# Feed-forward input in pairs of column blocks by seven block products, in a sequence written by hand

## The chip, the core and the metric

The kernel runs on one core of a Trainium2 chip. The metric is the device time of one execution in microseconds (us). The core's engines each work through a queue of their own, in order: TensorE (PE, with its weight loads as PEld), VectorE (DVE), ScalarE (ACT), GpSimd (POOL) and SyncE (SP, which only issues transfers here). They wait for each other by semaphores.

## What is computed

A layer of a decoder trunk, for one batch of 256 tokens:

```python
# S = 256 tokens, D = 1024, FFN_HIDDEN = 2816; one layer
xn = rmsnorm(h, norm_mix_g)
q_a, k_a, v_a, q_b, f_b, i_b, og_b, g_a, g_b = split_cols(xn @ w_in)     # nine blocks of 1024 columns
y_a = moba_attention(q_a, k_a, v_a, positions) @ w_br_attn               # 16 heads of 64, rotary, causal
y_b = hgrn2(q_b, f_b, i_b, og_b, lb, hgrn_norm_g) @ w_br_hgrn            # 8 heads of 128, gated recurrence
h = h + (sigmoid(g_a) * y_a + sigmoid(g_b) * y_b) @ w_out
h = h + memory_cross_attention(rmsnorm(h, norm_x_g), rmsnorm(mem, norm_mem_g), wq_x, wkv_x, wo_x)
hn = rmsnorm(h, norm_ffn_g)
gu = hn @ w_ffn_in                                                       # 1024 x 5632
h = h + (silu(gu[..., :2816]) * gu[..., 2816:]) @ w_ffn_out              # 2816 x 1024
return rmsnorm(h, final_norm_g)
```

## The kernel before

All weights are float32. For accuracy each matrix product is made of three: a weight chunk `raw` is split into a rounded part `hi` (ScalarE copies it to float32r) and a remainder `lo = raw - hi`, the activations likewise, and TensorE adds x_hi*w_hi, x_hi*w_lo and x_lo*w_hi in PSUM (`mm3t`, lines 236 to 239).

The weights are cut into 97 chunks of 1 MB (128 x 2048), laid out in DRAM in the order of their use (`plan`). `prep` loads a chunk on SP's queue into one of two `raw` buffers and splits it in two halves of 1024 columns: ScalarE makes `hi` (line 193); of `lo` (line 197) VectorE takes 576 columns of a half and GpSimd 448, but for the first nine chunks, where VectorE takes all. `nxt` hands out the next chunk and prepares two further ones; `hi` and `lo` have three buffers each. A chunk costs TensorE 24 matmuls of 512 columns.

Stages in order: the nine blocks of `w_in`, with recurrence and attention between them; the two branch outputs and `w_out`; cross-attention with `wkv_x`, `wq_x` and `wo_x`; the feed-forward, chunks 64 to 96. The last one's 2816 hidden columns are eleven blocks `o` of 256. Block `o` has two input chunks ("I", o, kh), one for each half kh of the 1024 features, each with 256 gate columns beside 256 value columns, and one output chunk ("O", o). For each token half t (128 tokens) the input chunks add into one PSUM bank `psi`; `gate` makes silu(r * gate) on ScalarE and the product with r * value on VectorE (`fu`), where r is the row scale of the norm. `turn_hid` turns the 256 x 256 block by four transposes into a bank `hidT` and splits it into `hid`, one of six buffers. `out_part` adds `hid` times the output chunk to four accumulators `acc`, which stay in PSUM to the end. Banks come from two pools of four: `mm` for psi, hidT and the like, `sm` for acc and smaller things. In the feed-forward the order on TensorE is I(o,0), turn(o-1), I(o,1), O(o-1):

```python
for u in ORDER[at[0]:-2]:
    if u[0] == "O":
        ffn_out(u[1])
        continue
    _, o, kh = u
    w = by_k(nxt(), 4)
    for t in range(2):
        ffn_in(o, kh, t, w)
        ...
        if kh == 1:
            gate(o, t)
    if kh == 0 and o:
        turn_hid(o - 1)
```

TensorE's queue stands as the code is written (a manual schedule). The other engines' queues are ordered by the scheduler from the code, except at the opening on GpSimd and in the closing sequence (final norm and output), which are written out by hand.

Of the kernel before, what the change touches and what calls it, by code (L numbers as in the profile page):

```python
# [10 lines left out]
F32 = mybir.dt.float32  # L11
F32R = mybir.dt.float32r
# [54 lines left out]


ORDER = plan()


def lay(ws):
# [45 lines left out]
def build(tc, A, out):  # L118
    nc = tc.nc
    V, SC, G, PE, SY = nc.vector, nc.scalar, nc.gpsimd, nc.tensor, nc.sync  # L120
    with ExitStack() as ctx:
# [14 lines left out]
        def t2(name, shape=(128, 512)):  # L136
            return ta.tile(list(shape), F32, name=name, tag="ta")
# [30 lines left out]
        def prep(tags=None, raw=None):  # L168
            i = made[0]
            made[0] += 1  # L170
            first = i < 2
            if raw is None:
                raw = wr.tile([128, 2048], F32, name="raw", tag="raw")
            if tags is None:
                hi = wh.tile([128, 2048], F32R, name="hi", tag="hi")
                lo = wl.tile([128, 2048], F32R, name="lo", tag="lo")
            else:
                hi = big(tags[0], "hix", (128, 2048), F32R)
                lo = big(tags[1], "lox", (128, 2048), F32R)
            pieces = 4 if first else 2  # L180
            n = 2048 // pieces
            sent = PIECES[i] if i < len(PIECES) else 1
            for c in range(sent if 0 < i < len(PIECES) else 0):
                a = slice(c * 2048 // sent, (c + 1) * 2048 // sent)
                SY.dma_start(raw[:, a], piece(A["w"][i], a))
            if sent == 1:
                SY.dma_start(raw, A["w"][i])
            for c in range(pieces):
                a = slice(c * n, (c + 1) * n)
                if i == 0:  # L190
                    SY.dma_start(raw[:, a], piece(A["w"][i], a))
                    yield
                SC.activation(hi[:, a], raw[:, a], AF.Copy)  # L193
                cut = (c + 1) * n - (0 if i in ALONE else POOL_COLS // pieces)
                for eng, b in ((V, slice(c * n, cut)), (G, slice(cut, (c + 1) * n))):
                    if b.start < b.stop:
                        eng.tensor_tensor(lo[:, b], raw[:, b], hi[:, b].bitcast(F32), op=ALU.subtract)  # L197
            ready[i] = (hi, lo)

        def run(g):  # L200
            for _ in g:
                pass

        def nxt(lead=LEAD):
            i = at[0]
            at[0] += 1
            while made[0] <= min(i + lead, len(ORDER) - 1):
                run(prep())
            return ready.pop(i)


# [24 lines left out]
        def mm3t(ps, xh, xl, h, l, first, last):  # L236
            PE.matmul(ps, xh, h, start=first, stop=False)  # L237
            PE.matmul(ps, xh, l, start=False, stop=False)  # L238
            PE.matmul(ps, xl, h, start=False, stop=last)  # L239

        def by_k(w, k):
            return tuple(t.rearrange("p (k c) -> p k c", k=k) for t in w)
# [819 lines left out]
        def wo_part(ps, t, c, kh):  # L1062
            t_part(ps, wo[2 * c + kh], (oxh, oxl), t, kh)

        def turn_h2(t, c):
# [7 lines left out]
            SC.activation(h2h[:, ks, ts], g, AF.Copy)  # L1073
            G.tensor_tensor(h2l[:, ks, ts], g, h2h[:, ks, ts].bitcast(F32), op=ALU.subtract)
# [12 lines left out]

        ring = ("B7", "B14", "B10", "B11", "B12", "B6")
        X2 = (h2h, h2l)
        hid, acc, two, psi, hm = {}, {}, {}, {}, {}  # L1090

        def gate(o, t):
            r, ps = two["r"][:, t:t + 1], psi.pop((o, t))
            g = t2("fg", (128, 256))
            SC.activation(g, ps[:, 0:256], AF.Silu, scale=r)  # L1095
            u = t2b("fu", (128, 256))
            V.scalar_tensor_tensor(u, ps[:, 256:512], r, g, op0=ALU.mult, op1=ALU.mult)  # L1097
            hm[o, t] = u

        def turn_hid(o):  # L1100
            bk = mm.tile([128, 2, 256], F32, name="hidT", tag="mm")
            for t in range(2):
                u = hm.pop((o, t))
                for j in range(2):
                    PE.transpose(bk[:, j, t * 128:(t + 1) * 128], u[:, j * 128:(j + 1) * 128], ident)
            hd = big(ring[o % 6], "hid", (128, 2, 2, 256), F32R)
            split(bk, hd[:, 0], hd[:, 1])
            hid[o] = hd

        def ffn_in(o, kh, t, w):  # L1110
            if kh == 0:
                psi[o, t] = mm.tile([128, 512], F32, name="psi", tag="mm")
            t_part(psi[o, t], w, X2, t, kh)

        def out_part(o, w, t, c, home=None, u=0, v=512):
            if home is None and (t, c) not in acc:
# [8 lines left out]
        def ffn_out(o):  # L1125
            w = by_k(nxt(), 2)
            for t in range(2):
                for c in range(2):
                    out_part(o, w, t, c)

        for u in ORDER[at[0]:-2]:
            if u[0] == "O":
                ffn_out(u[1])
                continue
            _, o, kh = u
            w = by_k(nxt(), 4)
            for t in range(2):
                ffn_in(o, kh, t, w)
                if (o, kh, t) == (0, 0, 0):
                    turn_h2(1, 1)  # L1140
                    two["r"] = rstd2(ssq2, "h2")
                if kh == 1:
                    gate(o, t)
            if kh == 0 and o:
                turn_hid(o - 1)

        n = NF // 2 - 1
        wa = by_k(nxt(), 2)  # L1150
        wb = by_k(nxt(), 2)
        out_part(n - 1, wa, 0, 0)
        turn_hid(n)
# [12 lines left out]
        hg3 = {i: big(ring[j], "hg3", (128, 512)) for j, i in enumerate(((0, 0), (0, 1), (1, 0)))}  # L1166
# [18 lines left out]
        def send(eng, t, u, w):  # L1185
            eng.dma_start(out[t * 128:(t + 1) * 128, u:w], H[:, t, u:w])

        E = mybir.EngineType
        with tc.manual_schedule(engines={E.Activation, E.DVE, E.Pool, E.SP}):
            add_out(acc[0, 0], 0, 0, 512)  # L1190
            mean_part(0, 0, 0, 512)
            gain(0, 0)
            add_out(acc[0, 1], 0, 512, 1024)
            mean_part(1, 0, 512, 1024)
            gain(0, 1)
            add_out(acc[1, 1], 1, 512, 1024)
            V.tensor_scalar(v3[:, 0:1], ssq3[:, 0:1], ssq3[:, 1:2], EPS, op0=ALU.add, op1=ALU.add)
            power(0, 0)
            SC.activation(H[:, 0, 0:512], hg3[0, 0], AF.Copy, scale=rs[0])
            send(SY, 0, 0, 512)  # L1200
            add_out(acc[1, 0], 1, 0, 512)
            mean_part(2, 1, 0, 512)
            gain(1, 0)
            for i in range(2):
                add_out(ends[i], 1, 512 + 256 * i, 768 + 256 * i)
                mean_part(3 + i, 1, 512 + 256 * i, 768 + 256 * i)
            V.tensor_scalar(H[:, 0, 512:1024], hg3[0, 1], rs[0], None, op0=ALU.mult)
            send(SY, 0, 512, 1024)
            V.tensor_scalar(v3[:, 1:2], ssq3[:, 2:3], ssq3[:, 3:4], EPS, op0=ALU.add, op1=ALU.add)
            V.tensor_scalar(v3[:, 2:3], ssq3[:, 4:5], v3[:, 1:2], None, op0=ALU.add)  # L1210
            power(1, 2)
            SC.activation(H[:, 1, 0:512], hg3[1, 0], AF.Copy, scale=rs[1])
            send(SC, 1, 0, 512)
            for i in range(2):
                a = slice(512 + 256 * i, 768 + 256 * i)
                V.scalar_tensor_tensor(H[:, 1, a], H[:, 1, a], rs[1], gfin[:, a], op0=ALU.mult, op1=ALU.mult)
                send(SY, 1, a.start, a.stop)


# [42 lines left out]
```

## Time and profile before

| | |
|---|---|
| device time, median of 3 runs | 626.13 us (625.99 to 626.78) |
| the profiled execution: span from first to last instruction | 624.0 us; the page gives no time of it beside the span |
| instructions in the span | 8466 |
| TensorE, weight loads | 615.9 us busy (99%), 512.5 us (82%) |
| VectorE, ScalarE, GpSimd | 384.2 us (62%), 331.4 us (53%), 372.4 us (60%) |
| moved by DMA | 107.50 MB, mean 172 GB/s |
| feed-forward on TensorE | from 432 us on |

A row of a group reads: line, engine, operation, output <- inputs, shapes, count, then busy us and mean ns of one, then the idle time of the engine just before them and what ended it. A row of a timeline or of the chain in order of time begins with its start and its length in us. A row of a table by stage has the stretch, the busy us (and instructions) of each engine, the granted clock, the DMA queues' share and GB/s. A matmul's record is its whole passage; the next one starts before it has ended.

### The profile page before, as it was taken

The page shows a single profiled execution, that of the slowest core. Times are in us where ns is not written, and L with a number is a line of the kernel's source. Part 1 is how long each engine was busy: PE and PEld are TensorE (multiplying, and loading weights), DVE is VectorE, ACT ScalarE, POOL GpSimd, SP SyncE. Part 2 cuts the span into 40 slices and gives each one's busy share as a digit, 9 for nine tenths or more (in the row PEclk, how much of TensorE's full clock was granted, in tenths as well). Part 3 has the DMA queues.
Part 4 walks back from the last instruction along what each step waited for, and adds up shares of the span by engine and source line. Part 5 has one row for each costly group of instructions (what it writes and reads, how often), then busy time and mean ns, then how long its engine had stood idle before and what let it go on. Part 6 is the DMA issues. An engine that isn't in the chain of part 4 may idle for free.

```text
span 624.0 us, 8466 instructions
## 1 busy us (share of the span) xinstructions
PE 615.9 (99%) x3135; PEld 512.5 (82%) x3135; DVE 384.2 (62%) x672; ACT 331.4 (53%) x533; POOL 372.4 (60%) x296
## 2 busy tenths in 40 slices
PE   9999999999999999999999999999999999999995
PEld 7888888888877877778888889888888888888884
DVE  7566678979766875748856456754444444444433
ACT  7775554234376756727457556644543444434432
POOL 3887844556544464355867876656655665566553
PEclk9999999999999999999999999999999999999998
DMA  9755443334443333545455544453344555454511
GB/s 345 296 204 202 155 182 135 135 135 140 185 149 135 136 135 134 204 169 183 156 207 189 183 175 189 140 199 134 132 178 171 195 203 187 166 190 198 203 68 67
DMA packets 16888, 107.50 MB, mean 172 GB/s; under 512 B 2000, under 2 KB 2640, under 8 KB 4560
## 3 DMA queue, kind: packets, MB, share of 16 engines
q1 hardware_dynamic: 16128, 106.14, 46.5%
q10 hardware_dynamic: 720, 0.84, 0.4%
q8 instruction: 24, 0.39, 0.3%
q14 instruction: 16, 0.13, 0.1%
HBM read 105.92 MB, written 1.05 MB: 171 GB/s over the span
## 4 chain that ended last, share of the span: by engine, by line
PE 98%; DVE 0%; POOL 0%; issue 0%; POOLq 0%; DVEq 0%
PE pst L237 14%; PE pst L239 14%; PE pst L238 14%; PE psi L237 6%; PE psi L239 6%; PE psi L238 6%; PE psf L252 5%; PE acc L237 3%; PE acc L239 3%; PE acc L238 3%; PE psf L253 2%; PE lp L616 2%; PE psg L510 1%; PE pso L237 1%; PE pso L239 1%; PE pso L238 1%
## 5 line engine op out<-in xcount | busy, mean ns | idle before, releaser
L197 POOL TENSOR_TENSOR lo<-raw,hi 128x448 fp32r<-128x448 f32 x172 | 272.6, 1602 | 182.1 <-ACT hi L193 169.6
L193 ACT ACTIVATE hi<-raw 128x1024 fp32r<-128x1024 f32 (+1 forms) x194 | 195.7, 1036 | 165.9 <-PE pst L239 58.9
L197 DVE TENSOR_TENSOR lo<-raw,hi 128x576 fp32r<-128x576 f32 (+2 forms) x194 | 198.1, 1027 | 133.6 <-ACT hi L193 131.6
L237 PE MATMUL pst<-hi,Xh 128*128 128x512 f32 x256 | 103.2, 403 | 0.0
L239 PE MATMUL pst<-hi,Xl 128*128 128x512 f32 x256 | 99.9, 390 | 0.0
L238 PE MATMUL pst<-lo,Xh 128*128 128x512 f32 x256 | 99.8, 390 | 0.0
L237 PE MATMUL psi<-hi,h2h 128*128 128x512 f32 x176 | 69.6, 395 | 0.0
L239 PE MATMUL psi<-hi,h2l 128*128 128x512 f32 x176 | 68.7, 390 | 0.0
L238 PE MATMUL psi<-lo,h2h 128*128 128x512 f32 x176 | 68.5, 389 | 0.0
L239 PEld LDWEIGHTS pst<-hi,Xl 128*128 128x128 f32 x256 | 48.0, 188 | 10.4
L237 PEld LDWEIGHTS pst<-hi,Xh 128*128 128x128 f32 x256 | 48.1, 188 | 9.9 <-issue 0.7
L238 PEld LDWEIGHTS pst<-lo,Xh 128*128 128x128 f32 x256 | 48.1, 188 | 9.3
L239 PEld LDWEIGHTS psi<-hi,h2l 128*128 128x128 f32 x176 | 33.0, 188 | 7.1
L238 PEld LDWEIGHTS psi<-lo,h2h 128*128 128x128 f32 x176 | 33.1, 188 | 6.6
L237 PEld LDWEIGHTS psi<-hi,h2h 128*128 128x128 f32 x176 | 33.1, 188 | 6.5
L237 PE MATMUL acc<-hi,hid 128*128 128x512 f32 x86 | 33.6, 390 | 0.0
L239 PE MATMUL acc<-hi,hid 128*128 128x512 f32 x86 | 33.5, 389 | 0.0
L238 PE MATMUL acc<-lo,hid 128*128 128x512 f32 x86 | 33.5, 389 | 0.0
L1097 DVE SCALAR_TENSOR_TENSOR fu<-psi,r_h,fg 128x256 f32<-128x256 f32 x22 | 10.6, 484 | 26.0 <-ACT fg L1095 26.0
L1095 ACT ACTIVATE fg<-psi,r_h 128x256 f32<-128x256 f32 x22 | 10.4, 475 | 29.9 <-PE psi L239 29.9
L252 PE MATMUL psf<-H,hi 128*128 128x512 f32 x64 | 22.8, 400 | 0.0
L252 PE MATMUL psf<-M,hi 128*128 128x512 f32 x64 | 22.5, 396 | 0.0
(344 smaller groups left out, 1120.9 us busy)
## 6 DMA issues: line engine op xcount, KB each, us to landing
raw<-w SPq DMA_DIRECT2D x94, 1024.0 KB, 4.8
raw<-w SPq DMA_DIRECT2D x4, 512.0 KB, 6.1
raw<-w SPq DMA_DIRECT2D x4, 256.0 KB, 4.1
H<-xtok SPq DMA_DIRECT2D x1, 1024.0 KB, 9.2
mraw<-mT SPq DMA_DIRECT2D x1, 1024.0 KB, 5.0
xraw<-xT SPq DMA_DIRECT2D x1, 512.0 KB, 6.1
gfin<-gfin SPq DMA_DIRECT2D x1, 512.0 KB, 3.7
out<-H SPq DMA_DIRECT2D x2, 256.0 KB, 2.0
```

The lines of the kernel that those rows point to most:

```text
L193: SC.activation(hi[:, a], raw[:, a], AF.Copy)
L197: eng.tensor_tensor(lo[:, b], raw[:, b], hi[:, b].bitcast(F32), op=ALU.subtract)
L237: PE.matmul(ps, xh, h, start=first, stop=False)
L238: PE.matmul(ps, xh, l, start=False, stop=False)
L239: PE.matmul(ps, xl, h, start=False, stop=last)
L252: PE.matmul(ps, w[0][:, k, a], X2[:, :, k], start=k == 0, stop=False)
L253: PE.matmul(ps[:, 0], w[1][:, k, a], X2[:, 0, k], start=False, stop=k == 7)
L510: PE.matmul(pss[c][t], z[:, k, t * 128:(t + 1) * 128], ws[c][0][:, k], start=z is Xh and k == 0, stop=False)
L616: PE.matmul(ps[:, j], KS[:, a0 + j], QQ[:, a0 + j, 0:n], start=True, stop=True)
L1095: SC.activation(g, ps[:, 0:256], AF.Silu, scale=r)
L1097: V.scalar_tensor_tensor(u, ps[:, 256:512], r, g, op0=ALU.mult, op1=ALU.mult)
```

## The change

*Seven products for a pair.* Block 0 stays as it was. The ten others go in pairs (a, b). The input of a pair is a product of 2 x 2 blocks: two token halves by two feature halves, times two feature halves by two column blocks. Eight block products of 12 matmuls (four 128-deep steps of three) become seven: products 1 and 2 are x(0, k) times W(a, k) for token half 0; products 5, 6 and 7 use sums of weight chunks and sums of token blocks, 4 and 3 the last sum of each side beside a plain one. Product 1's result is kept, 6, 7 and 4 are added onto it in the same bank, and what stands there after 1, 6 and 7 is copied out by ScalarE (`copied`), since three of the four results are such copies with product 2 added, or 5, or 5 and 3, subtracted by VectorE (`into`); the fourth is the bank after product 4.

*Weight sums.* For each pair two chunk-sized sums, W(b,0) + W(a,0) and W(b,0) + W(b,1), are made in HBM while the earlier stages run: a plain copy issued by ScalarE and an accumulating transfer issued by GpSimd (`block_sums`, one step at every second chunk from 6 to 38 and from 52 to 56). The third is a VectorE addition of two loaded chunks (`third_sum`), the fourth an accumulating transfer of W(a,1) into that third one in SBUF, once it has been split (`fourth_sum`). The token sums are four VectorE additions and their splits, once.

*The stage in a hand-written sequence.* `FFN` lists the steps; a step is a chunk of 24 matmuls (I, O) or a product of 12 (P). For the first pair the order is 1, 2, 6, 5, 7, O, 4, 3, for the others 1, 2, 5, 6, O, 7, O, 4, 3. At the start of step k, `ahead(k)` puts into the queues of ScalarE, VectorE, GpSimd and SP, in this order: what follows from the step before (`posts`: copies, gates, hidden splits), the load of step k+5, the third sum and the split of step k+3, the accumulate of step k+2. All `lo` of the feed-forward are VectorE's. There are four `hi`/`lo` buffers and up to seven `raw`. Gates: ScalarE scales both halves, GpSimd multiplies. From chunk 36 on VectorE takes all of `lo` in the earlier stages, too (`SHARED`).

*Banks by hand.* The four `mm` banks are taken once (`four`): numbers 0 and 2 change places from pair to pair as the banks of products 1 and 2, number 3 is for product 5, and number 1 is for every `turn_hid`. The hidden blocks live in a ring of four in one tile. The two last output parts (`ends`) are in two of the four banks, and the last output chunk's split has own buffers. The table load for silu is moved ahead of the stage.

```diff
-ALONE = range(9)
+SHARED = range(9, 36)
+HEAD = [i for i, u in enumerate(ORDER) if u[0] not in "IO"]
+PAIRS = [(o, o + 1) for o in range(1, NF // 2, 2)]
+def feed_forward():
+    out = [("I", 0, 0), ("I", 0, 1)]
+    for g, (a, b) in enumerate(PAIRS):
+        names = (1, 2, 5, 6, a - 2, 7, a - 1, 4, 3) if g else (1, 2, 6, 5, 7, 0, 4, 3)
+        outs = (4, 6) if g else (5,)
+        out += [("O", n) if i in outs else ("P", g, n) for i, n in enumerate(names)]
+    return out + [("O", o) for o in PAIRS[-1]]
+AHEAD = 5
...
+        def block_sums():
+            for g, (a, b) in enumerate(PAIRS):
+                for i in range(2):
+                    tc.keep_in_program_order(SC.dma_start(summed[g][i], A["w"][AT_CHUNK["I", b, 0]]))
+                    yield 1
+                for i, u in enumerate((("I", a, 0), ("I", b, 1))):
+                    tc.keep_in_program_order(G.dma_start(
+                        summed[g][i], A["w"][AT_CHUNK[u]], accum_op=ALU.add, max_dma_last_dim=8192))
+                    yield 1
...
+        def third_sum(k):
+            if k < len(FFN) and FFN[k][0] == "P" and FFN[k][2] == 6:
+                g = FFN[k][1]
+                raw_of[g, "u"] = raws.pop(0)
+                for c in range(2):
+                    a = slice(c * 1024, (c + 1) * 1024)
+                    V.tensor_tensor(raw_of[g, "u"][:, a], raw_of[g, "t"][:, a], raw_of[g, "b"][:, a], op=ALU.add)
+        def fourth_sum(k):
+            if FFN[k][0] == "P" and FFN[k][2] == 6:
+                g = FFN[k][1]
+                G.dma_start(raw_of[g, "u"], A["w"][AT_CHUNK["I", PAIRS[g][0], 1]], accum_op=ALU.add)
...
+        def product(ps, p, w, first):
+            xh, xl = left(p)
+            for k in range(4):
+                mm3t(ps, xh[:, k], xl[:, k], w[0][:, k], w[1][:, k], first and k == 0, k == 3, not first)
+        def copied(ps):
+            c = t2("fc")
+            SC.activation(c, ps, AF.Copy)
+            return c
+        def gate(o, t, src):
+            r = two["r"][:, t:t + 1]
+            g = t2("fg", (128, 2, 256))
+            SC.activation(g[:, 0], src[:, 0:256], AF.Silu, scale=r)
+            SC.activation(g[:, 1], src[:, 256:512], AF.Copy, scale=r)
+            u = pt.tile([128, 256], F32, name="fu", tag="pt")
+            G.tensor_tensor(u, g[:, 0], g[:, 1], op=ALU.mult)
...
         def turn_hid(o):
-            bk = mm.tile([128, 2, 256], F32, name="hidT", tag="mm")
+            bk = four[1].rearrange("p (a b) -> p a b", a=2)
...
+        def ahead(k):
+            todo = list(posts)
+            posts.clear()
+            for f in todo:
+                f()
+            fetch(k + AHEAD)
+            third_sum(k + 3)
+            parts(k + 3)
+            if k + 2 < len(FFN):
+                fourth_sum(k + 2)
...
+            if p == 2:
+                posts.append(lambda to=to: gate(a, 0, into(cs[1], to, ALU.add)))
+            elif p == 7:
+                posts.append(lambda b5=banks[5]: gate(b, 1, into(cs[7], b5, ALU.subtract)))
+            elif p == 4:
+                posts.append(lambda to=to: gate(a, 1, to))
+            elif p == 3:
+                posts.append(lambda to=to: gate(b, 0, into(cs[6], to, ALU.subtract)))
...
+            elif p in (1, 2):
+                posts.append(turn_hid(a - 3 + p))
...
-        ends = [mm.tile([128, 256], F32, name="end", tag="mm") for _ in range(2)]
+        ends = [four[2 * i][:, :256] for i in range(2)]
```

*TensorE at a turn of the hidden block, before.* `hidT` is a bank out of the pool, between two input chunks:

```order
L239 MATMUL psi_4631<-hi_4533,h2l_3871 128x512
L1105 MATMUL hidT_4644<-cst_90,fu_4556 128x128 x2
L1105 MATMUL hidT_4644<-cst_90,fu_4572 128x128 x2
L237 MATMUL psi_4618<-hi_4575,h2h_3870 128x512
L238 MATMUL psi_4618<-lo_4576,h2h_3870 128x512
```

*The same engine now, at the start of the third pair:* the end of product 1 (into bk_4026), the first turn, and the start of product 2 (into bk_4024). bk_4025 is the bank of every turn:

```order
L274 MATMUL bk_4026<-hl_3851,h2l_3847 128x512
L1248 MATMUL bk_4025<-cst_90,fu_4385 128x128 x2
L1248 MATMUL bk_4025<-cst_90,fu_4534 128x128 x2
L272 MATMUL bk_4024<-hi_4513,h2h_3846 128x512
L273 MATMUL bk_4024<-lo_4514,h2h_3846 128x512
L274 MATMUL bk_4024<-hi_4513,h2l_3847 128x512
```

After nine further rows of product 2, which repeat these three, the second turn stands ahead of product 5 (into bk_4027, with the token sums Sh):

```order
L273 MATMUL bk_4024<-lo_4514,h2h_3846 128x512
L274 MATMUL bk_4024<-hi_4513,h2l_3847 128x512
L1248 MATMUL bk_4025<-cst_90,fu_4559 128x128 x2
L1248 MATMUL bk_4025<-cst_90,fu_4481 128x128 x2
L272 MATMUL bk_4027<-hi_4537,Sh_4021 128x512
L273 MATMUL bk_4027<-lo_4538,Sh_4021 128x512
```

The two turns of a pair now stand twelve matmuls apart, both into one bank; before, 72 matmuls lay between turns, each into a bank from the pool.

*VectorE at one block, before:* splits (`lo`), the hidden block's split (`hid`), the gates' products (`fu`):

```order
L197 TENSOR_TENSOR lo_4576<-raw_4574,hi_4575 128x576 x2
L197 TENSOR_TENSOR lo_4610<-raw_4608,hi_4609 128x576 x2
L197 TENSOR_TENSOR lo_4654<-raw_4652,hi_4653 128x576
L279 TENSOR_TENSOR hid_4649<-hidT_4644,hid_4649 128x512
L197 TENSOR_TENSOR lo_4654<-raw_4652,hi_4653 128x576
L1097 SCALAR_TENSOR_TENSOR fu_4676<-psi_4618,r_h2_4067,fg_4674 128x256
```

*The same engine now, at the start of the third pair:* product 5's split, the bank sum for product 3 of the pair before (`fc`), the third weight sum (into raws_3848), product 6's split, the hidden block (`hids`) out of the bank of the turns, the next output chunk's split, the bank sum for product 2, the second hidden block:

```order
L1171 TENSOR_TENSOR lo_4538<-raw_4016,hi_4537 128x1024 x2
L1285 TENSOR_TENSOR fc_4423<-bk_4027,fc_4423 128x512
L1148 TENSOR_TENSOR raws_3848<-raw_4016,raw_4015 128x1024 x2
L1171 TENSOR_TENSOR lo_4565<-raws_3848,hi_4564 128x1024 x2
L314 TENSOR_TENSOR hids_4020<-bk_4025,hids_4020 128x512
L1171 TENSOR_TENSOR hl_3852<-raw_4017,hl_3851 128x1024 x2
L1285 TENSOR_TENSOR fc_4586<-bk_4024,fc_4586 128x512
L314 TENSOR_TENSOR hids_4020<-bk_4025,hids_4020 128x512
```

The split that frees the bank of the turns stands behind two splits, a bank sum and a weight sum; the halves of a split are 1024 columns wide instead of 576.

More of the change, by code (lines that the diff above doesn't have):

```diff
@@ L202, in run @@
                 pass
+        dram = pool("dram", 1, space=bass.MemoryType.DRAM)
+        summed = [[dram.tile([128, 2048], F32, name="sum%d_%d" % (g, i), tag="sum%d_%d" % (g, i))
+                   for i in range(2)] for g in range(len(PAIRS))]
+        def block_sums():
[7 more added lines that the diff above has]
+                    yield 1
+        sums = block_sums()
         def nxt(lead=LEAD):
@@ L206, in nxt @@
             at[0] += 1
-            while made[0] <= min(i + lead, len(ORDER) - 1):
+            while made[0] <= min(i + lead, len(HEAD) - 1):
                 run(prep())
+            if i % 2 == 0 and (6 <= i < 40 or i > 50):
+                next(sums, 0)
             return ready.pop(i)
@@ L234, in mm3, with mm3t @@
             PE.matmul(ps, ll, rh, start=False, stop=last)
[L236 to L239, printed above, removed]
+        def mm3t(ps, xh, xl, h, l, first, last, more=False):
+            PE.matmul(ps, xh, h, start=first, stop=False, skip_group_check=more)
+            PE.matmul(ps, xh, l, start=False, stop=False, skip_group_check=more)
+            PE.matmul(ps, xl, h, start=False, stop=last, skip_group_check=more)
         def by_k(w, k):
@@ L1072, in turn_h2 @@
             V.tensor_tensor(g, bk, bc(gv[:, V_FFN + 4 * c:V_FFN + 4 * c + 4], 128, 2), op=ALU.mult)
-            SC.activation(h2h[:, ks, ts], g, AF.Copy)
-            G.tensor_tensor(h2l[:, ks, ts], g, h2h[:, ks, ts].bitcast(F32), op=ALU.subtract)
+            split(g, h2h[:, ks, ts], h2l[:, ks, ts])
+            gh[t, c] = g
+        X2 = (h2h, h2l)
+        hid, acc, two, psi, hm = {}, {}, {}, {}, {}
+        two_raw = big("P0", "raws", (128, 2, 2048))
+        raws = [wr.tile([128, 2048], F32, name="raw", tag="raw") for _ in range(2)] + [two_raw[:, i] for i in range(2)]
@@ L1085, in build @@
                 todo = (t, c)
[L1088 to L1097, printed above, removed]
+        for k in range(3):
+            parts(k)
@@ L1123, in out_part @@
                      (o == 0 or home is not None) and k == 0, k == 1 and o >= NF // 2 - (2 if t and c else 1))
[L1125 to L1131, printed above, removed]
-            if u[0] == "O":
-                ffn_out(u[1])
-                continue
[L1135 to L1145, printed above, removed]
+        E = mybir.EngineType
@@ new lines, in build @@
+        region = tc.manual_schedule(engines={E.Activation, E.DVE, E.Pool, E.SP})
+        region.__enter__()
+        posts, banks, cs = [], {}, {}
+        def ahead(k):
[8 more added lines that the diff above has]
+                fourth_sum(k + 2)
+        four = [mm.tile([128, 512], F32, name="bk", tag="mm") for _ in range(4)]
@@ new lines, in into @@
+        def into(c, b, op):
+            V.tensor_tensor(c, b, c, op=op)
+            return c
+        half8 = None
+        for k, u in enumerate(FFN[:-2]):
+            if u[0] == "I":
+                ahead(k)
+                w = use(k)
+                for t in range(2):
+                    if k == 0:
+                        psi[t] = four[(1, 3)[t]]
+                    t_part(psi[t], w, X2, t, u[2])
+                    if (k, t) == (0, 0):
+                        turn_h2(1, 1)
+                        two["r"] = rstd2(ssq2, "h2")
+                        token_sums()
+                    if k == 1:
+                        posts.append(lambda t=t: gate(0, t, psi[t]))
+                if k == 1:
+                    sum_parts(1, 0)
+                continue
+            ahead(k)
+            w = use(k)
+            if u[0] == "O":
+                o = u[1]
+                half = o == PAIRS[-1][0] - 1
+                for t in range(1 if half else 2):
+                    for c in range(2):
+                        out_part(o, w, t, c)
+                if half:
+                    half8 = w
+                continue
+            g, p = u[1:]
+            a, b = PAIRS[g]
+            if p in (1, 2, 5):
+                banks[p] = four[3 if p == 5 else (0, 2)[(g + p) % 2]]
+            to = banks[{1: 1, 6: 1, 7: 1, 4: 1, 2: 2, 5: 5, 3: 5}[p]]
+            product(to, p, w, p in (1, 2, 5))
+            if p in (1, 6, 7):
+                posts.append(lambda p=p, to=to: cs.update({p: copied(to)}))
+            if p == 2:
[6 more added lines that the diff above has]
+                posts.append(lambda to=to: gate(b, 0, into(cs[6], to, ALU.subtract)))
+            if g == 0:
+                if p == 2:
+                    posts.append(turn_hid(0))
+                elif p in (6, 5):
+                    sum_parts(2 if p == 6 else 3)
+            elif p in (1, 2):
+                posts.append(turn_hid(a - 3 + p))
@@ L1186, in send @@
             eng.dma_start(out[t * 128:(t + 1) * 128, u:w], H[:, t, u:w])
[L1188 to L1217, printed above, removed]
@@ L1220 @@
+        send(SC, 1, 0, 512)
+        for i in range(2):
+            a = slice(512 + 256 * i, 768 + 256 * i)
+            V.scalar_tensor_tensor(H[:, 1, a], H[:, 1, a], rs[1], gfin[:, a], op0=ALU.mult, op1=ALU.mult)
+            send(SY, 1, a.start, a.stop)
+        region.__exit__(None, None, None)
 def kernel(**inputs):
```

128 lines of the change are left out of this document (117 added, 11 removed).

## The prediction

> **What bounds the kernel now.** I read the page first (busy time, chain of waits, queues), then the core's granted clock, the table by stage, the chain in order of time near the end, the groups of instructions with their shapes kept apart, and the timelines of VectorE.
>
> ```profile
> span 624.0 us, 8466 instructions
> PE 615.9 (99%) x3135; PEld 512.5 (82%) x3135; DVE 384.2 (62%) x672; ACT 331.4 (53%) x533; POOL 372.4 (60%) x296
> PE 98%; DVE 0%; POOL 0%; issue 0%; POOLq 0%; DVEq 0%
> core 0: 624.0 us, clock 0.997
> 432.00:606.00 174.00, 174.00 (x790) 144.00 (x789) 79.01 (x95) 76.62 (x95) 103.89 (x64) 1.00 0.47 176
> ```
>
> The chain that ended last is TensorE for 98%, at full clock. In the last row, the feed-forward stage (432 to 606 us), TensorE is busy all 174 us, VectorE 79, ScalarE 77, GpSimd 104. So what is taken from TensorE here comes off the time, until another queue makes TensorE wait.
>
> The price of a matmul has two readings:
>
> ```profile
> L239 PE MATMUL psi<-hi,h2l 128*128 128x512 f32 x176 | 68.7, 390 | 0.0
> 607.41 0.44 PE hidT L1105 x4
> 611.27 0.23 PE acc L237
> ...
> 615.35 0.23 PE acc L237
> ```
>
> The group's mean says 390 ns, but matmuls overlap: between the two acc rows lie 18 starts in 4.08 us, 0.2267 us each. That is the price: a product of 12 matmuls takes 2.72 us, an input or output chunk of 24 takes 5.44, four transposes 0.44.
>
> **The change part by part.** *Removed on TensorE.* Five pairs had 96 input matmuls each and get 7 x 12 = 84: 60 fewer, 60 x 0.2267 = 13.6 us, all on the path. Transposes, output matmuls and the closing sequence keep their number. A pair now takes 7 x 2.72 + 2 x 5.44 + 0.87 = 30.8 us of TensorE instead of 33.5.
>
> *Load of the other engines.* Each product has its own weight chunk to split, so ScalarE and VectorE split nine chunks in 30.8 us where they split six in 33.5, and GpSimd splits none.
>
> ```profile
> L193 ACT ACTIVATE hi<-raw 128x1024 fp32r<-128x1024 f32 x186 | 190.9, 1054 | 163.8 <-PE pst L239 58.9 <-PE psi L239 35.5 <-PE acc L239 28.1
> L278 ACT ACTIVATE hid<-hidT 128x512 fp32r<-128x512 f32 x11 | 6.4, 583 | 1.3 <-PE hidT L1105 1.3
> L1095 ACT ACTIVATE fg<-psi,r_h 128x256 f32<-128x256 f32 x22 | 10.4, 475 | 29.9 <-PE psi L239 29.9
> L975 ACT ACTIVATE ku<-psf 128x256 f32<-128x256 f32 x16 | 6.0, 374 | 1.0 <-PE psf L253 0.9
> 24.48 2.49 DVE L197 TENSOR_TENSOR lo<-raw,hi 128x1024 fp32r<-128x1024 f32 x2 [1.76 <-ACT hi L193]
> L279 DVE TENSOR_TENSOR hid<-hidT,hid 128x512 fp32r<-128x512 f32 x11 | 7.5, 686 | 1.4 <-ACT hid L278 1.4
> L1172 DVE TENSOR_TENSOR H<-acc,H 128x512 f32<-128x512 f32 x4 | 2.8, 692 | 4.7 <-PE acc L239 4.7
> L979 POOL TENSOR_TENSOR kxl<-kx,kxh 128x256 fp32r<-128x256 f32 x8 | 5.8, 737 | 1.5 <-ACT kxh L978 1.5
> ```
>
> ScalarE per pair: 18 halves x 1.05 + three bank copies and two hidden splits x 0.58 + four gates x (0.475 + 0.374) = 25.2 us. VectorE: the row at 24.48 gives 1.245 us a half (two in 2.49); 18 halves + 2 for the third weight sum + three bank sums x 0.69 + two hidden splits x 0.69 = 28.3. GpSimd: four multiplies x 0.74 = 3.0 and one DMA. So on the mean TensorE still ends last, with 2.5 us over VectorE. Queues are in order, though, and products 4, 3, 1, 2, 5, 6 stand in a row, six short steps; there a wait can open.
>
> *The new wait: one bank for the turned hidden block.* Before, that bank came from the pool of four; now both blocks of a pair turn through number 1 of the four, after products 1 and 2. The second four transposes must wait until VectorE has taken the first from the bank, and that subtraction stands behind the splits of the next weights. I count from the end of product 4. ScalarE reads its bank first: 0.16 for the matmul's tail (0.39 - 0.23), 0.475 + 0.374, then a half's split 1.05: 2.1 us. Then VectorE in its order: product 5's two halves 2.49, the bank sum of the previous product 3 0.69, the third weight sum 2.49, product 6's halves 2.49, the hidden block 0.69: 8.85, or 8.2 where instructions in a row overlap by some 0.1 us. The bank is free 10.3 to 10.9 us after product 4. TensorE needs product 3, product 1, four transposes and product 2: 3 x 2.72 + 0.44 = 8.60. The wait is 1.7 to 2.3 us; I take 2.0. It occurs in pairs 2 to 5, since the first pair turns one block: 8.0 us.
>
> In the first pair product 7 adds onto the bank of product 6, and ScalarE must copy out of it during the one product (5) between them. ScalarE has 4.7 us queued there (gate 0.85, hidden split 0.58, a chunk 2.1, token sum 0.58, copy 0.58), begun some 1.5 us after product 6 started, against 5.44: 0.6 us, with 0 and 2.7 (a whole product) as ends. Elsewhere an output chunk of 5.44 lies between.
>
> *Weight sums.* Ten copies (ScalarE's queue) and ten accumulates (GpSimd's) in HBM are issued during the earlier stages, five accumulates into SBUF in the feed-forward. No such transfer is in the trace of before.
>
> ```profile
> raw<-w SPq DMA_DIRECT2D x94, 1024.0 KB, 4.8
> H<-xtok SPq DMA_DIRECT2D x1, 1024.0 KB, 9.2
> GB/s 345 296 204 202 155 182 135 135 135 140 185 149 135 136 135 134 204 169 183 156 207 189 183 175 189 140 199 134 132 178 171 195 203 187 166 190 198 203 68 67
> ACT hi L193 <- PE pst L239: 58.9, 19, 4.7
> ACT hi L193 <- DMA raw<-w: 13.3, 6, 4.9
> ```
>
> In the earlier stages the weight splits mostly wait for TensorE to free a buffer (58.9 us), seldom for their load (13.3 us, some of it at the start). The loads move 135 to 204 GB/s there where the queues reached 345. One more MB every second chunk fits into that; I take 0 us, with 0 and 10 us as ends (each of the 20 holding TensorE up by 0.5 us).
>
> The accumulate into SBUF reads 1 MB from HBM and 1 MB that is already there, and writes 1 MB: a load's 4.8 us plus another 1.05 MB at 345 GB/s (3.0) is 7.8 us; the ends are 4.8 (as a load) and 18.4 (twice the crowded 9.2). It can't start before product 6's halves are split, about 9.6 us after product 4. ScalarE gets to the sum after the copy of product 6: 8.60 + 2.0 wait + 0.44 + 2 x 2.72 = 16.5 to the end of product 6, then 0.8 for tail and copy and the chunk still queued ahead, 2.1: 19.4. So 9.8 us are covered, and 7.8 fits. Beyond that ScalarE stands, and with it the splits and copies queued behind.
>
> The fetches themselves, 38 instead of 33, are 7 MB a pair in 32.8 us, 224 GB/s, with the accumulate still under 345.
>
> *GpSimd's share given to VectorE* (chunks 36 on). Beside a busy GpSimd 576 columns cost VectorE more than they do alone:
>
> ```profile
> 506.74 0.76 DVE L197 TENSOR_TENSOR lo<-raw,hi 128x576 fp32r<-128x576 f32 x1 [0.46 <-ACT hi L193]
> 507.69 1.44 DVE L197 TENSOR_TENSOR lo<-raw,hi 128x576 fp32r<-128x576 f32 x1 [0.19 <-ACT hi L193]
> L197 DVE TENSOR_TENSOR lo<-raw,hi 128x576 fp32r<-128x576 f32 x172 | 175.0, 1020 | 125.9 <-ACT hi L193 124.1
> ```
>
> The mean is 1.02 us, so 1024 columns at 1.24 cost 0.2 more a half, and the part that GpSimd took last, 1.6 us, is gone. 0 us, hidden under 5.44 a chunk; ends -1 and +2. The last output parts in two of the four banks, the hidden ring in one tile and the moved table load (1.28 us on ScalarE, off the chain) are 0 as well.
>
> *A rule against the change.* VectorE's halves slow by 1.34 (1.02 over 0.76) beside a splitting GpSimd. The Trainium skill, GPSIMD Engine Reference, section Specifications, says that GpSimd shares its SBUF interfaces with VectorE and contends with instructions that have two SBUF inputs, and every split and sum here is one; the two rows above agree. By it at its full size the six halves of the new wait cost 2.5 us more a pair; by the share of time that GpSimd is left busy (3 of 31 us) next to nothing.
>
> **Sum.** -13.6 + 8.0 + 0.6 = -5.0 us. Span 624.0 to 619.0; the page gives the span alone, and the runs' median of 626.13 stands 2.1 over it, so 621.1.
>
> **The rivals.**
> 1. *No bank wait:* overlap and a ScalarE that runs ahead hide all of it. For it: the margin is only 1.7 to 2.3 us of 11. 626.1 - 13.6 = 612.5.
> 2. *The accumulate lands late.* At 12 us instead of 7.8, ScalarE stands 12 - 9.8 = 2.2 us in each of five pairs, +11: 632. It costs the whole gain from 10.8 us on. For it: H's load took 9.2 among others, and a pair's loads fill two thirds of the queues. Against it: 94 loads have a median of 4.8. The Trainium skill, DMA: Bandwidth & Descriptors, section on queues, rings and completion order, says that each DMA engine goes round its queues packet by packet, so a load beside the accumulate would halve its rate; no run here shows it for two queues.
> 3. *VectorE becomes the bound* through GpSimd's multiplies and descriptor work: 20 halves x 1.245 x 1.34 + 3.5 = 36.8 us a pair against 32.8, +4.0 x 5 - so 641 at full size, 626 at a quarter. Against it: GpSimd is busy a tenth of the time.
> 4. *The HBM sums hold up the earlier stages:* up to +10, 631.
> 5. *The products don't shorten TensorE's queue:* excluded, the order has 60 rows fewer.
>
> **How the numbers follow.** Measured runs differ by 0.8 us, so 0.2% (1.25 us) is about what can be told from no change: faster is under 624.9, slower over 627.4. The forecast of 619 to 623 has 0.46; 1 and what lies between it and the forecast 0.20; 2 has 0.17, of which 0.03 near no change; 3 0.08, of which 0.03 near no change; 4 and the rest 0.09, of which 0.03 is near no change and 0.02 still faster. Faster 0.68, same 0.09, slower 0.23. The range runs from rival 1 to rival 2, 612.5 to 632; the forecast's own is 618 to 624.
>
> **What would show it.** Right: 3075 matmuls in a span near 619; waits of TensorE's loads on the hidden split, four times about 2 us, after product 2; VectorE busy nine tenths in the feed-forward; the accumulate landing within 10 us. Wrong: ScalarE's splits waiting for the accumulate; TensorE waiting for low halves; a stage before 432 us that grew; halves on VectorE near 1.6 us.

## The result: 1.2% slower, and the profile after

The changed kernel takes 634.03 us (median of 4 runs, 631.04 to 635.65) against 626.45 us for the kernel before beside it: ratio 1.0119, 95% interval 1.0092 to 1.0146. The forecast was 621.1 with a range of 612.5 to 632. The profiled execution took 635.65 us with a span of 633.9, the longest of the four; it had 9.9 us more span than the one before.

The page's opening lines and its chain of waits, which answer to the first ones of before:

```profile
span 633.9 us, 8404 instructions
PE 612.3 (97%) x3075; PEld 506.2 (80%) x3075; DVE 460.2 (73%) x717; ACT 379.8 (60%) x605; POOL 203.3 (32%) x207
PE 62%; DMA 12%; DVE 10%; POOL 7%; ACT 4%; issue 3%; SPq 0%; ACTq 0%; POOLq 0%; DVEq 0%
```

The 60 matmuls are gone (3075 where there were 3135), but the chain, 98% TensorE before, now runs for 36% through transfers, VectorE, GpSimd, ScalarE and issue gaps: TensorE waits. The table by stage of the changed kernel, cut where its feed-forward starts and where its last matmul ends (columns: length, then busy time of PE, PEld, DVE, ACT, POOL, granted clock, queues' share, GB/s):

```profile
0.00:437.30 437.30, 432.86 (x2289) 359.68 (x2290) 315.23 (x568) 253.54 (x428) 171.03 (x174) 1.00 0.67 227
437.30:627.20 189.90, 179.45 (x787) 146.51 (x785) 142.81 (x144) 124.59 (x173) 31.03 (x32) 0.96 0.62 204
```

The same cuts in the kernel before are at 432.0 and 617.5:

```profile
432.00:617.50 185.50, 185.46 (x847) 153.54 (x845) 83.50 (x103) 80.46 (x105) 107.68 (x68) 1.00 0.44 165
```

So the stages ahead of the feed-forward grew by 5.3 us, and the feed-forward itself, from which 13.6 us of matmuls were taken, grew by 4.4: 18.0 us went into waits and into a lower granted clock (0.96 of full speed on the mean of the stage). These are figures of the slowest of the four executions; the median is 1.6 us shorter. The waits of TensorE in the changed kernel (total, times, longest):

```profile
PE bk L1248 <- DVE hids L314: 8.1, 4, 2.0
PE bk L272 <- ACT fc L1231: 2.1, 1, 2.1
...
PE aT L826 <- DVE ap L818: 1.5, 1, 1.5
```

The first is the one bank for the turned blocks, the second is product 7 of the first pair waiting for the copy of product 6, the third lies in the attention at 255 us. And the clock: three windows laid on the moments at which the granted clock changed, around the wait of the first pair, and two around the wait of the fourth pair (the granted clock is the third number from the end, TensorE's busy time the first one after the length):

```profile
459.52:462.93 3.41, 1.35 (x6) 0.53 (x4) 3.15 (x4) 3.35 (x5) 0.15 (x1) 1.00 1.01 382
462.93:466.35 3.42, 3.10 (x8) 2.44 (x8) 3.31 (x5) 3.42 (x5) 0.00 (x0) 0.50 1.00 395
466.35:469.76 3.41, 3.41 (x16) 2.80 (x16) 2.86 (x3) 1.41 (x4) 0.00 (x0) 1.00 0.97 317
...
551.68:555.09 3.41, 1.77 (x8) 1.13 (x6) 3.34 (x4) 3.33 (x6) 0.82 (x1) 1.00 0.65 190
555.09:558.51 3.42, 3.04 (x16) 2.61 (x17) 3.10 (x4) 1.08 (x2) 0.89 (x1) 1.00 0.90 199
```

After a window in which TensorE was idle for 2.06 us (3.41 - 1.35), the clock is 0.50 for exactly one window: 8 matmuls instead of 16, so 1.7 us are lost beyond the wait. In the fourth pair a wait of the same length fell across a boundary, 1.64 us on one side and 0.37 on the other, and the clock stayed. Four waits of the feed-forward were followed by such a window: 4 x 1.7 = 6.8 us. With 8.1 + 2.1 + 0.3 us of waits that makes 17.3 of the 18.0; the remaining 0.7 us is not traced to a cause.

### The profile page after: what moved, and what is told of

The parts are those of the page before. It is cut to its first block, busy times and chain, and to the rows that moved or that the text cites. A ratio compares the mean times of both kernels' runs of the same rounds, so it can differ in the third digit from the quotient of the medians.

```text
span 633.9 us, 8404 instructions
## 1 busy us (share of the span) xinstructions
PE 612.3 (97%) x3075; PEld 506.2 (80%) x3075; DVE 460.2 (73%) x717; ACT 379.8 (60%) x605; POOL 203.3 (32%) x207
## 4 chain that ended last, share of the span: by engine, by line
PE 62%; DMA 12%; DVE 10%; POOL 7%; ACT 4%; issue 3%; SPq 0%; ACTq 0%; POOLq 0%; DVEq 0%
DMA raw<-w 10%; PE pst L272 8%; PE pst L274 8%; PE pst L273 8%; PE psf L287 5%; PE bk L274 4%; PE bk L273 4%; PE bk L272 4%; PE acc L274 3%; PE acc L272 3%; PE acc L273 3%; DVE lo L214 3%; PE psf L288 2%; DVE lo L1171 2%; ACT hi L210 2%
## 5 line engine op out<-in xcount | busy, mean ns | idle before, releaser
L214 DVE TENSOR_TENSOR lo<-raw,hi 128x1024 fp32r<-128x1024 f32 (+2 forms) x128 | 149.1, 1181 | 73.9 <-ACT hi L210 73.7
L210 ACT ACTIVATE hi<-raw 128x1024 fp32r<-128x1024 f32 (+1 forms) x128 | 128.1, 1028 | 115.5 <-DMA raw<-w 60.3
L214 POOL TENSOR_TENSOR lo<-raw,hi 128x448 fp32r<-128x448 f32 x54 | 77.3, 1455 | 53.9 <-ACT hi L210 52.2
L1171 DVE TENSOR_TENSOR lo<-raw,hi 128x1024 fp32r<-128x1024 f32 x54 | 64.6, 1238 | 17.0 <-ACT hi L1170 16.6
L1170 ACT ACTIVATE hi<-raw 128x1024 fp32r<-128x1024 f32 x54 | 54.4, 1053 | 10.9 <-DVE raw L1148 5.2
L272 PE MATMUL bk<-hi,Sh 128*128 128x512 f32 x64 | 27.1, 424 | 2.1 <-ACT fc L1231 2.1
L274 PE MATMUL bk<-hi,Sh 128*128 128x512 f32 x64 | 26.9, 421 | 0.3 <-DVE Sh L314 0.3
L273 PE MATMUL bk<-lo,Sh 128*128 128x512 f32 x64 | 26.6, 415 | 0.0
L272 PE MATMUL bk<-hi,h2h 128*128 128x512 f32 x60 | 23.7, 395 | 0.0
L274 PE MATMUL bk<-hi,h2l 128*128 128x512 f32 x60 | 23.4, 390 | 0.0
L273 PE MATMUL bk<-lo,h2h 128*128 128x512 f32 x60 | 23.4, 389 | 0.0
```

Of the source, the lines that this page charges most:

```text
L272: PE.matmul(ps, xh, h, start=first, stop=False, skip_group_check=more)
L273: PE.matmul(ps, xh, l, start=False, stop=False, skip_group_check=more)
L274: PE.matmul(ps, xl, h, start=False, stop=last, skip_group_check=more)
L1171: V.tensor_tensor(lo[:, a], raw[:, a], hi[:, a].bitcast(F32), op=ALU.subtract)
```

## Experiments

The theory at the start had three parts: the bank wait, the half clock behind each long wait, and the transfers of the HBM sums holding up the stages before. Rivals: the waits are only visible parts of something else, and the earlier stages grew because VectorE took over GpSimd's share of the split.

**The second turn one product later.** All matmuls stay; only the place of four transposes moves.

```diff
-            elif p in (1, 2):
-                posts.append(turn_hid(a - 3 + p))
+            elif p in (1, 5):
+                posts.append(turn_hid(a - 2 if p == 1 else a - 1))
```

> Edit: in pairs 2 to 5 the second hidden block is turned after product 5 instead of after product 2, so one more product (2.72 us) lies between the two uses of bank 1. Theory A (the bank wait costs itself and a clock drop behind it): the four waits on the hidden split (8.7 us over the bare rate in the profiled run) go, and with them the half-clock windows behind three of them (3 x 1.6 = 4.9 us): 634.0 - 13.6 = 620.4, and no granted clock under 1.00 in pairs 2 to 5. Rival (the waits alone cost time; the products of 0.43 us behind them have another cause): 634.0 - 8.7 = 625.3, the slow products stay. Rival (the wait only moves, to product 6 or to the output chunk behind it): 629 to 634.

Measured: 622.16 us (620.84 to 622.41), ratio to the kernel before 0.9925 (0.9913 to 0.9938): from 1.2% slower to 0.75% faster. Its waits of TensorE:

```profile
PE bk L272 <- ACT fc L1231: 2.1, 1, 2.1
...
PE bk L1248 <- POOL fu L1240: 1.0, 1, 1.0
```

The row on the hidden split is gone. The clock was halved only twice, behind the first pair's wait and at the end. Of the 1.8 us short of the forecast, 1.0 is a new wait in the closing sequence, where a turn now comes before GpSimd's product is ready. This wait of 0.9 to 1.5 us stands in every profile with the later turn and in none with the earlier one.

**TensorE kept busy during the wait.** Eight matmuls that nothing reads stand ahead of the second transposes, so the bank comes free no earlier.

```diff
             elif p in (1, 2):
+                if p == 2:
+                    xh, xl = left(p)
+                    for j in range(8):
+                        PE.matmul(four[3], xh[:, j % 4], w[0][:, j % 4], start=j == 0, stop=j == 7)
                 posts.append(turn_hid(a - 3 + p))
```

> Eight matmuls (8 x 0.2267 = 1.81 us) that nothing reads are put between product 2 and the second four transposes in pairs 2 to 5, into the bank that product 5 starts afterwards: TensorE computes during most of the wait, and the bank comes free no earlier. Theory A (a wait of some 2 us within one window of 3.41 us halves the granted clock for the next window): waits on the hidden split fall to some 0.4 us each, the granted clock stays at 1.00 behind them, and only the 3 x 1.6 us of half clock are saved: 634.0 - 4.9 = 629.1. Rival (the slow products behind the wait come from something else, such as operands or memory): they stay at 0.43 us and the time stays at 634, or grows by what of the eight matmuls doesn't fit into the wait (up to 4 x 0.2).

Measured: 629.51 us (628.16 to 632.2), ratio 1.0062 (1.0044 to 1.008): 4.5 us less than the changed kernel, with 32 matmuls more. Its waits and two windows around the second pair's:

```profile
PE bk L1248 <- DVE hids L314: 0.8, 4, 0.2
```

```profile
484.00:486.00 2.00, 1.79 (x11) 1.27 (x10) 2.00 (x4) 1.19 (x2) 0.91 (x1) 1.00 0.77 315
486.00:488.00 2.00, 2.00 (x10) 1.64 (x9) 1.52 (x2) 0.45 (x2) 0.00 (x0) 1.00 0.96 156
```

Useless work in the place of idle time keeps the clock at 1.00 in pairs 2 to 5, and the products behind it run at full rate. In the two profiled executions the feed-forward's excess falls by 4.6 us, against 3 x 1.6 forecast: the half clock follows from TensorE's idle time, and not from what the products behind the wait read.

**The HBM sums left out.**

```diff
-                next(sums, 0)
+                pass
```

(and the loads of the sums take weight chunks)

> Leaves out part of the computation: the ten copies and ten accumulates in HBM are not issued, and the feed-forward loads plain weight chunks of the same size in the place of the sums, so the output differs. Theory A (these transfers delay the weight loads, ScalarE stands in its queue behind a late load, and the attention steps behind it hold up TensorE): the feed-forward starts near 432 us again instead of 437.3 and the time is 634.0 - 5.3 = 628.7; the feed-forward itself is as long as in the changed kernel. Rival B (the stages before grew because VectorE took GpSimd's share of the low halves from chunk 36 on): the start stays at 437 and the time at 634.

Measured: 631.11 us (630.75 to 631.37), ratio 1.0077 (1.0065 to 1.0089). The first matmul of its feed-forward:

```profile
432.96 0.39 PE L272 MATMUL bk<-hi,h2h 128*128 128x512 f32 x1
```

That is 437.33 in the changed kernel and 431.95 before. So the transfers are a condition of the late start. The median fell by 2.9 us and not by the 5.3 of Theory A, which was taken from the slowest execution of the changed kernel. The rival was not out yet: it could be that both are needed. Copies and accumulates were not left out singly.

**GpSimd's share of the split given back.**

```diff
-SHARED = range(9, 36)
+SHARED = range(9, 64)
```

> GpSimd again splits 448 of 1024 columns in chunks 36 to 63, as before the change; all else is the changed kernel. Rival B (the moved share made the jump of 3.4 us at chunk 36): the feed-forward starts near 433 and the time is about 630. Theory A (late loads did): the start stays within 1 us of 437.3 and the time within 1 us of 634.0.

Measured: 631.38 us (629.41 to 632.02), ratio 1.0078 (1.0066 to 1.009), and the start:

```profile
433.69 0.39 PE L272 MATMUL bk<-hi,h2h 128*128 128x512 f32 x1
```

Here my theory gave 634 and was wrong: with all twenty transfers in place the start comes back as far as without them. But not for the rival's reason, as GpSimd's queue shows. In the changed kernel, the two accumulates of the fourth pair's sums:

```profile
236.80 1.77 POOL L231 DMA_DIRECT2D sum<-w  x2
```

and in this run:

```profile
245.77 0.88 POOL L231 DMA_DIRECT2D sum<-w  x1
260.48 0.82 POOL L231 DMA_DIRECT2D sum<-w  x1
```

The code calls for one at every second chunk. With the splits of chunks 36 on taken out of GpSimd's queue, nothing stood between the two, and both left at once, some 9 and 23 us early. What that does, by the changed kernel's queues between 225 and 262 us (packets, MB, share of 16 engines) and its chain in order of time:

```profile
q1 hardware_dynamic: 693, 5.02, 37.3%
q0 software_dynamic: 288, 2.10, 28.7%
```

```profile
238.41 12.49 DMA raw<-w
251.01 1.07 ACT hi L210
252.10 1.23 DVE lo L214
...
255.31 1.13 DVE lo L214
...
257.23 1.49 PE aT L826 x6
```

The load issued at 238.41 takes 12.49 us instead of some 5; with GpSimd's share given back, the load of the same moment took 4.7. ScalarE, whose queue has its split next, stands for 6.2 us with the attention's exponentials behind it; VectorE's normalisation comes late, TensorE waits 1.5 us for it (third row of its waits) and then gets a window at half clock (258.13 to 261.55). The feed-forward is late by 3.7 us from this place alone: TensorE is 1.2 us behind the kernel before ahead of it and 4.9 us behind it afterwards. The split given back to GpSimd is worth a little besides: at 407 us TensorE loses 0.6 us in the changed kernel, waiting for a normalisation that stands behind VectorE's wider half, and nothing in this run.

**Pace without the work.** GpSimd splits 16 columns instead of 448, VectorE 1008.

```diff
-                cut = (c + 1) * n - (POOL_COLS // pieces if i in SHARED else 0)
+                cut = (c + 1) * n - (POOL_COLS // pieces if i in SHARED else 32 // pieces if i >= 36 else 0)
```

> In chunks 36 to 63 GpSimd splits 16 of 1024 columns, VectorE the other 1008: VectorE's work is that of the changed kernel, but GpSimd's queue has an entry for every half again, between which its accumulates stand. Theory P (without these entries GpSimd's queue ran ahead and started two accumulates 0.6 us apart at 237 us, beside three loads): the two start 15 to 20 us apart, the feed-forward starts at 433 to 434 instead of 437.3, and the time is that of the run with GpSimd's whole share, 631.4. Rival L (VectorE's larger share of the split delays the attention steps): start 437 and 634.

Measured: 631.66 us (630.5 to 632.86), ratio 1.0078 (1.0062 to 1.0094), the same as with the whole share. Its accumulates:

```profile
246.41 0.89 POOL L231 DMA_DIRECT2D sum<-w  x1
260.33 0.83 POOL L231 DMA_DIRECT2D sum<-w  x1
```

Theory P holds: VectorE's load is that of the changed kernel, only the pace is back, and the jump at 250 us is gone. The profiles of all runs, those of the later experiments with them, agree on it. In the four in which nothing stands between the two accumulates, they leave 0.6 us apart, the load behind them takes 12.0 to 12.5 us, and TensorE falls 1.6 to 3.7 us further behind, the 3.7 where a halved window followed; in the seven other kernels TensorE loses nothing there against the kernel before. The start, 434.9, was 1 us later than forecast, from two small losses elsewhere (1.7 us at 140 us and 1.2 us at 407 us).

**The twenty transfers in the kernel before**, at the same chunks, with their result unused; `block_sums` and its `dram` tiles are those of the change.

```diff
             while made[0] <= min(i + lead, len(ORDER) - 1):
                 run(prep())
+            if i < 64 and i % 2 == 0 and (6 <= i < 40 or i > 50):
+                next(sums, 0)
```

> The kernel before with the twenty transfers of the HBM sums added at the same chunks, their result unused. Theory P (the transfers hurt where nothing paces them; here GpSimd splits in every chunk): the feed-forward starts at most 1 us after 432, time 626.2 to 627.2. Rival (20 MB more through the queues cost time whatever their pace): start at 436 to 437, time 630 to 631.

Measured: 628.22 us (627.11 to 633.04), ratio 1.0033 (1.0018 to 1.0049); the start is at 432.9, 0.9 us late. The start is as P had it; the median is 1 us above P's range and 1.8 below the rival's. So paced transfers cost 1 to 2 us, not 4 to 5. ScalarE's wait in this run between 45 and 430 us:

```profile
ACT hi L193 <- DMA raw<-w: 49.9, 14, 8.1
```

That is almost as long as in the changed kernel (57.5 us, 13 times). Most of ScalarE's waiting for loads is thus harmless. At 250 us it cost time because something that TensorE needed soon was queued behind it.

**The bank sum ahead, in the first pair.** On top of the later turn, VectorE does the bank sum of product 2 ahead of a chunk's halves instead of behind them.

```diff
+            if u == ("P", 0, 2):
+                flush()
+                banks[2] = four[0]
+                product(banks[2], 2, use(k), True)
+                early = into(cs[1], banks[2], ALU.add)
+                ahead(k)
+                posts.append(lambda: gate(PAIRS[0][0], 0, early))
+                posts.append(turn_hid(0))
+                continue
...
```

The reason, from ScalarE's timeline in the changed kernel:

```profile
457.94 0.51 ACT L1237 ACTIVATE fg<-fc,r_h 128x256 f32<-128x256 f32 x1 [2.22 <-DVE fc L1285]
...
461.65 0.58 ACT L1231 ACTIVATE fc<-bk 128x512 f32<-128x512 f32 x1
```

> On top of the turn after product 5 (622.2): in the first pair VectorE does the bank sum of product 2 ahead of the splits of one chunk instead of behind them; one row moves in VectorE's queue, none elsewhere. Theory C (ScalarE stood 2.2 us for that bank sum, with the copy of product 6 queued behind it, and TensorE waited for that copy and then ran a window of 3.41 us at half clock): the excess of 4.5 us in the first pair falls under 1, no clock under 1.00 there, 622.2 - 4 = 618.2. Rival (the copy is late for ScalarE's own load, 4.7 us of work in its queue): excess 4 to 4.5, 622.

Measured: 622.45 us (621.82 to 625.99), ratio 0.9944 (0.9923 to 0.9966), no gain over 622.16. Its waits:

```profile
PE bk L1248 <- DVE hids L314: 2.1, 2, 1.9
...
PE bk L274 <- DVE Sh L314: 0.7, 1, 0.7
```

Theory C was right on the mechanism, since the wait for the copy (L1231) and its half clock are gone and 0.7 us is left. But TensorE then ran into the bank wait in the second pair, earlier than before, and the window behind it was halved: 3.6 us given back.

**Three edits together, a still later turn, and another spread.** First the later turn, the bank sum ahead and GpSimd's share together; then the second turn after product 6; then, besides, one transfer at every third chunk.

```diff
-            elif p in (1, 5):
+            elif p in (1, 6):
...
-            if i % 2 == 0 and (6 <= i < 40 or i > 50):
+            if i == 4 or i % 3 == 0 and i >= 3:
                 next(sums, 0)
```

> The turn after product 5, the bank sum ahead in the first pair, and GpSimd's share of the split in chunks 36 to 63 as before the change, together. If the causes add up: 618.2 less the 2.4 us of start that the share was worth, 615.8. If a new wait takes their place (VectorE is busy some nine tenths of a pair, and the last turn waited 1.1 us for GpSimd's product): 617 to 620.

> The three edits of the run before (619.3), with the second hidden block turned after product 6 instead of 5. If the wait of 2.0 us left in the second pair and the half clock behind it (3.8 us together) hang on the use of bank 1 alone, they go: 615.5, and 11.4 us fewer than the kernel before at TensorE's full clock. Rival (ScalarE and VectorE are still behind from the first pair, so the next consumer waits instead: product 7 for the copy of product 6, or the output chunk for the hidden block's halves): 617 to 619.5.

> The kernel of the run above, with the twenty transfers issued one at every third chunk from chunk 3 on, in place of every second one up to 40 and above 50. If the 1.0 to 1.3 us by which the feed-forward still starts late come from loads beside transfers that follow each other closely, a third of them goes: up to 1 us less than the run above. If each transfer costs the same wherever it lies, no difference; chunks from 38 to 50 follow each other more closely (5.5 us instead of 7), so it can also be up to 2 us slower.

Measured, in this order: 619.26 us (618.87 to 619.93), ratio 0.9883 (0.9866 to 0.99); 617.81 us (617.03 to 620.16), ratio 0.9882 (0.9862 to 0.9902); 623.63 us (623.04 to 624.49), ratio 0.9961 (0.9949 to 0.9974). The first two beat both kernels, the one before by some 1.2% and the changed one by some 2.4%; the difference between them can't be told from these runs, though the profiled spans are 618.1 and 616.0. Both came out as their second forecasts had it: new waits took the place of the old ones. The third lies outside its range, which ended 2 us above the second. In the second one's profile, TensorE has no halved window left:

```profile
span 616.0 us, 8488 instructions
PE 603.8 (98%) x3075; PEld 500.6 (81%) x3075; DVE 453.7 (74%) x717; ACT 376.5 (61%) x605; POOL 296.4 (48%) x263
```

```profile
PE bk L1248 <- POOL fu L1240: 1.5, 1, 1.5
PE bk L272 <- ACT fc L1231: 1.0, 1, 1.0
PE rT L786 <- POOL ra L781: 0.8, 1, 0.8
PE bk L274 <- DVE Sh L314: 0.7, 1, 0.7
```

So 8.0 of the 13.6 us have arrived. The 0.9 us of late start, nearly all of it the third row's wait at 140 us, and the 3.2 us of the other three rows make 4.1 of the 5.6 that are missing; 1.5 us is not traced. The spread at every third chunk, meant as a small gain, costs 5.8 us: it puts transfers beside chunks 38 to 50, which TensorE uses in 5.5 us each, and there, from 305 to 316 us, TensorE fell 4 us further behind. ScalarE stood up to 9.3 us for one load there. In these two kernels the number of transfers is the same; their places make the difference.

## Why the prediction was wrong

*Removed on TensorE, -13.6:* right. *Load of the other engines:* right; VectorE's busy time in the feed-forward is 142.8 us, five pairs of 28.3 being 141.5, and its halves take 1.24 us:

```profile
L1171 DVE TENSOR_TENSOR lo<-raw,hi 128x1024 fp32r<-128x1024 f32 x54 | 64.6, 1238 | 17.0 <-ACT hi L1170 16.6
```

So rival 3, at 1.34 times that, did not come; GpSimd's multiplies took 0.99 instead of 0.74 us, and no wait of TensorE for them shows in the changed kernel.

*The bank wait, 8.0:* 8.1 us, in the four places foretold, here in the second pair:

```profile
486.10 0.63 PE L1248 MATMUL bk<-cst,fu 128*128 128x128 f32 x4 [2.03 <-DVE hids L314]
```

The mechanism was right: from product 5's split to the hidden block, VectorE's queue took 8.65 us there (477.31 to 485.96), where the count had 8.2 to 8.85. That the sum agrees to 0.1 us is partly luck, since each wait was placed between 1.7 and 2.3 us; the three other profiles with the unfilled early turn have 8.5 to 8.8.

*The step that was missing:* the sum took a wait at its length. Each wait of 2 us that lies within one clock window costs 1.7 more. The trace of before shows full clock until its last matmul, and TensorE's only wait there is one of 1.6 us at the very start, so it had no row for this. It was 6.8 us in the feed-forward, and with it alone the forecast of -5.0 becomes a loss of 1.8. The Trainium skill, TensorE: Matmul & The Clock Gate, section Part 1: The HAM clock gate, says that the clock is set by activity in a free-running window of 3413 ns and that an idle window halves it. The window agrees (3.41 us). Its advice to avoid gaps above some 3.4 us is not enough here: 2.0 us sufficed.

*The first pair, 0.6:* 2.1 us, within its ends of 0 and 2.7 (1.5 + 4.7 - 5.44 of its own working is 0.8, not 0.6). The step "begun some 1.5 us after product 6 started" failed: ScalarE began 3.5 us after (457.94 against 454.48), since it stood 2.2 us for a bank sum that was queued behind four halves on VectorE. I had walked through ScalarE's queue, but not through the queue of the engine for which it waits.

*The HBM sums, 0:* 3.2 to 5.4 us of late start in the four profiles with this placement and without the pacing splits, within the ends of 0 and 10 and as rival 4 had it, to which I gave 0.09 together with the rest. The failed step is "one more MB every second chunk fits": it fits on the mean and paced, at 1 to 2 us. The share taken from GpSimd was costed at 0 for VectorE; it was 0.6 us at 407 us (1.2 in one profile), and it was never looked at as what paced GpSimd's accumulates. Each term alone left the start some 1 to 2 us late, both together 3 to 5 us.

*The accumulate into SBUF, 7.8 with 9.8 covered:* it landed later, after 9.4 and 9.7 us, and in three pairs the cover was 8.8 us, so that ScalarE stood for it 1.0, 1.0 and 0.5 us. The landings and two of these waits:

```profile
raw<-w POOLq DMA_DIRECT2D x4, 1024.0 KB, 9.4
raws<-w POOLq DMA_DIRECT2D x1, 1024.0 KB, 9.7
...
495.56 2.01 ACT L1170 ACTIVATE hi<-raw 128x1024 fp32r<-128x1024 f32 x2 [1.04 <-DMA raw<-w]
530.23 2.01 ACT L1170 ACTIVATE hi<-raws 128x1024 fp32r<-128x1024 f32 x2 [0.97 <-DMA raws<-w]
```

No wait of TensorE followed, so rival 2 did not come. The loads issued some 2.5 us behind an accumulate took 8.3 to 8.9 us, where the fastest loads of the stage took 4.7.

The profiled span by these terms: -13.6 + 8.1 + 2.1 + 6.8 + 5.3 = 8.7 of 9.9 us. The 5.3 is for the most part 1.0 at 140 us, 3.7 at 250 and 0.6 at 407. What stays open is the loss at 140 us, 0 to 1.7 us in the profiles with the transfers.

## What to carry to other kernels

Where an engine that never waited is about to wait, add to each wait what it does to the clock, and break a wait that can't be removed, or fill it: four waits of 2 us cost 13 here with the three halved windows behind them, and one more product between two uses of a bank took nearly all of it back. Work moved off a queue also takes away what spaced the transfers issued from it; look for what follows on that queue. And of a wait on engine A for engine B, walk through B's queue too before writing down when A starts.

## What was not expected of the hardware

The half clock has a sharp edge. Over all traces, 26 windows of the feed-forward had over 1.3 us without a matmul: laid on the 3.41 us grid of each trace's clock changes, eleven with 1.32 to 1.90 us idle were followed by full clock, fifteen with 1.87 to 2.81 us by half clock. The edge lies near 1.9 of 3.41 us. One window in the attention, with transposes in it, was halved after 1.54 us. So the same program loses 1.7 us or nothing by where a wait falls on the grid, and the four executions of the changed kernel, which differ by 4.6 us, are slower in the order in which their mean granted clock is lower: 0.992, 0.988, 0.986, 0.984.

An accumulate of 1 MB keeps the queues busy far longer than a load: by the rows of 225 to 262 us, two took 28.7% of 37 us, 5.3 us of all sixteen engines each, against 2.9 us for a load of the same size (37.3% of 37 us for 5.02 MB). Over the whole changed kernel the queues give 5.5 us for each of the fifteen accumulates and 2.8 us for a load.
